# Memory layout of W_pe and p^T: one consecutive piece for each load

## The chip, the core and the metric

The kernel runs on one core of a Trainium2 chip. The metric is the device time of one execution in microseconds (us), lower is better. The core has a matrix engine (PE in the profile, its weight loads PEld), a vector engine (DVE), a scalar engine (ACT), a general engine (POOL), and SP, which here only issues DMAs. ACT can issue DMAs too. Every engine works through its own list of instructions in a fixed order and waits on semaphores for the others. PE reads its operands from on-chip memory (SBUF) and writes its sums to a second on-chip memory (PSUM), which the other engines read.

## The reference

One layer (DEPTH = 1) over 1024 tokens of 1024 numbers, in float32. What the change touches is the term with `p` and `w_ple_proj` (W_pe) in the last lines:

```python
h = rms_norm(x, norm_mix_g); proj = h @ w_in          # q, k, v, gates, conv inputs
o = gla_chunked(q, k, v, gk)                          # chunked gated linear attention
y_a = (rms_norm(o, gla_norm_g) * silu(z_a)) @ w_branch_a
u = causal_dwconv(cc * xc, conv_w)
y_c = (cb * u * silu(z_c)) @ w_branch_c
x = x + (sigmoid(g_a + b_ga) * y_a + sigmoid(g_c + b_gc) * y_c) @ w_out
ple_gate = sigmoid(rms_norm(x, norm_ple_g) @ w_ple_gate)
x = x + ple_gate * (p @ w_ple_proj)                   # p: 1024 x 256, w_ple_proj: 256 x 1024
return rms_norm(x, norm_final_g)
```

## The kernel before

Every float32 product is split into a high and a low part of a faster format (`split`, line 614: ACT casts the high part, DVE subtracts it for the low part) and made of three matmuls: high x high, high x low, low x high (`mm3`, line 625). The large products are further cut down by a seven-product scheme (class `Cell`, line 741). The program is not written in the order in which it runs. The functions note operations (`Flow.note`, line 260), and a planner (`set_dues`, `put_in_order`, lines 362 and 409) puts them in order for each engine by costs, latencies and due times; `nc.hurry` moves a due time forward. The cost of a DMA to the planner depends on its bytes alone. All operations are issued from line 520, so in the profile nearly every row carries L520 and is told apart by its tile's name.

The first thing that the kernel computes is the product p W_pe (`pe` in the profile), because it needs nothing but two small inputs: W_pe and p^T, 256 x 1024 each, 1 MB each. It is kept in memory (`ped`) until the last stage of the kernel, which loads it back and multiplies it by the gate. Eight matmuls on constants (`warm`, line 1049) run on PE while the first loads are on their way.

Before the change `_lay_out` (line 1839, on the host) hands both over as arrays of 128 x 2 x 1024: for each of the 128 rows of SBUF, the two blocks (`kt` = 0, 1) of 1024 numbers. Row after row is 8 KB on in memory, and a load of some columns of one block takes from each row a piece of 1 KB or 2 KB. The loads are, in the order of the program (lines 1069 to 1082; `first` names the first three pieces):

- two quarters of block 0, columns 0 to 255 and 256 to 511 (1 KB a row, 128 KB a load), W_pe's from ACT's queue, p^T's from SP's;
- block 1, columns 0 to 511 (2 KB a row, 256 KB), of W_pe and then of p^T, from SP's queue; called piece (1, first half) below;
- the second halves of W_pe's two blocks, from SP's queue;
- two loads of x^T (`hq`), then the second halves of p^T's two blocks, then two more of x^T.

The tiles that receive them are `wperaw` and `pTraw`; the split parts are `wpehi`, `wpelo`, `pThi` and `pTlo`. `pe_blocks` (line 1137) makes the products for token blocks 0 to 3 and the first 512 columns in two steps: first everything with block `kt` = 0, in the order of the quarters, for all four token blocks; then the rest with `kt` = 1, which needs the pieces (1, first half).

In the last stage (`make_gate`, line 1732) one part of p W_pe is computed a second time for the last rows instead of being loaded: `get` (line 1797) loads columns 256 to 511 of W_pe and the last 128 columns of p^T again into `pwraw`, splits them into `pwhi` and `pwlo`, and `piece` (line 1739) multiplies them into `pelast`. In the program and on SP's queue these loads stand some 66 us before their use.

Of the kernel before, what the change touches and what calls it, by code (L numbers as in the profile page):

```python
# [16 lines left out]
P = 128  # L17
# [519 lines left out]
def kernel(  # L537
# [4 lines left out]
    wb: bass.AP,  # L542
    wgl: bass.AP,
    wgk2: bass.AP,
    wpe: bass.AP,
    pT: bass.AP,
    xT: bass.AP,
    vecs: bass.AP,
    gbc: bass.AP,
# [3 lines left out]
    nc = Flow(tc)  # L553
# [57 lines left out]
    load = nc.sync.dma_start  # L611
    store = nc.sync.dma_start

    def split(hi, lo, src):

        nc.scalar.copy(hi, src)
        tt(lo, src, f(hi), op=ALU.subtract)
# [37 lines left out]
    def slot(k, s, name, shape=(4, 512), dtype=F32R):  # L655
        return rp.tile([P, *shape], dtype, tag=f"r{k}{s}", name=name)
# [84 lines left out]
    class Cell:  # L741
# [10 lines left out]
        def load(self, k):  # L752
            for n in NEED[self.side][k]:
                if self.raw[n] is None and not (self.fresh and k == 1 and n == 3):
                    self.raw[n] = bp.tile([P, 4, P], F32, tag="raw", name=f"{self.name}raw{n}", bufs=8)
                    load(self.raw[n], self.src[n])
            if k == 1 and self.s1 is not None and self.seed is None:
                self.seed = bp.tile([P, 512], F32, tag="raw", name=f"{self.name}s1", bufs=8)
                load(self.seed, self.s1)
# [142 lines left out]
    def rows(b):  # L902
        return slice(b * P, (b + 1) * P)
# [148 lines left out]
    with phase("prep0") as pool:  # L1052
        pr_ = slot(4, "h", "pTraw", (2, SEQ), F32)
        wr_ = slot(4, "l", "wperaw", (2, D), F32)
        halves = [slice(hh * 512, (hh + 1) * 512) for hh in range(2)]
# [7 lines left out]
        def get_x(i):  # L1063
            for n in (0, 3) if i == 0 else (1, 2):
                for kp in range(0, 4, 2):
                    kk = 4 * quad[n][1] + kp
                    load(q[n][:, kp:kp + 2, :], xT[:, kk:kk + 2, halves[i]])
# [2 lines left out]
        first = [(0, slice(0, 256)), (0, slice(256, 512)), (1, halves[0])]  # L1070
        for n, (kt, cs) in enumerate(first):
            nc.hurry = 14.0 - 2.0 * n
            (nc.scalar if kt == 0 else nc.sync).dma_start(wr_[:, kt, cs], wpe[:, kt, cs])
            load(pr_[:, kt, cs], pT[:, kt, cs])
        nc.hurry = 8.0
        for kt in range(2):
            load(wr_[:, kt, halves[1]], wpe[:, kt, halves[1]])
        nc.hurry = 0.0
        get_x(0)
        load(vec, vecs)  # L1080
        for kt in range(2):
            load(pr_[:, kt, halves[1]], pT[:, kt, halves[1]])
        get_x(1)
        load(trim, tri)

# [280 lines left out]
    with phase("conv", [ph["qk"]]) as vp:  # L1366
# [26 lines left out]
        for g in range(4):  # L1393
            t, u = [], []
# [269 lines left out]
    with phase("late", [ph["sw"], ep]) as lp:  # L1664
# [63 lines left out]
        with phase("fin", [ph["sw4"]], lp) as gp:  # L1728
# [3 lines left out]
            def make_gate(p, cell):  # L1732
# [56 lines left out]
                def late_cons(i, j, src):  # L1789
                    if not xt:  # L1790
                        get()
                    piece(i, slice(512 * j, 512 * j + 512), src, i ^ j, i != j)
# [4 lines left out]
                def get():  # L1797
                    for i in range(2):
                        xt.append(lp.tile([P, D], F32, tag="x", name=f"x3_{p}_{i}", bufs=4))
                        load(xt[i], x2d[2 * p + i])  # L1800
                        ms.append(sm.tile([P, 2], F32, tag="ms3", name=f"ms3_{p}_{i}", bufs=4))
                    if p == 3:
                        raw = gp.tile([P, 2, P + 256], F32, name="pwraw")
                        load(raw[:, :, 0:P], pT[:, :, rows(7)])
                        load(raw[:, :, P:], wpe[:, :, 256:512])
                        pw.extend(gp.tile([P, 2, P + 256], F32R, name=f"pw{s}") for s in ("hi", "lo"))
                        split(*pw, raw)

                def cons(i, j, src):
                    if p == 3 or p == 2 and i == 1:  # L1810
                        return late_cons(i, j, src)
                    if not xt:
                        get()
                    js = slice(j * 512, (j + 1) * 512)
                    t = gp.tile([P, 512], F32, tag="pe", name=f"pe{p}_{i}_{j}", bufs=4)
                    load(t, ped[2 * p + i][:, js])
                    act(src, src, AF.Sigmoid, scale=rgate[p, i][:, 0:1])
                    tt(t, src, t, op=ALU.mult)
                    tt(xt[i][:, js], xt[i][:, js], t, op=ALU.add)
                    act(junk[:, 0:512], xt[i][:, js], AF.Square, scale=1.0 / 32.0, accum_out=ms[i][:, j:j + 1])  # L1820
                    seen[i] += 1
                    if seen[i] == 2:
                        r = rstd_of(ms[i][:, 0:1], f"rf{p}_{i}", ms[i][:, 1:2])
                        stt(xt[i], xt[i], r[:, 0:1], gf, op0=ALU.mult, op1=ALU.mult)
                        store(out[rows(2 * p + i), :], xt[i])
# [13 lines left out]
def _lay_out(inp):  # L1839

    import numpy as np

    a = {n: np.asarray(v) for n, v in inp.items()}
    w = a["w_in"][0]
    o = np.cumsum([0, 512, 512, 1024, 1024, 16, 1024, 1024, 1024, 1024, 1024, 1024])
    q, k, v, za, gl, cb, cc, xc, zc, ga, gc = (w[:, o[i]:o[i + 1]] for i in range(11))
    col = lambda m, n: m[:, n * 256:n * 256 + 256]
    cells = []
    for hp in range(2):
        cells += [col(q, hp), col(k, hp)]  # L1850
    cells += [col(za, h) for h in range(4)]
    for g in range(4):
        cells += [col(m, g) for m in (cc, xc, zc, cb)]
    for m in (ga, gc, a["w_branch_c"][0], a["w_branch_a"][0]):
        cells += [col(m, c) for c in range(4)]

    def quads(m):
        n = m.shape[1] // 2
        t = lambda r, c: m[r * 512:r * 512 + 512, c * n:c * n + n].reshape(4, 128, n).transpose(1, 0, 2)
        return t(0, 0), t(0, 1), t(1, 1), t(1, 0)  # L1860

    wc = np.stack([np.stack([np.stack(quads(m)[0:2], 1), np.stack(quads(m)[2:4], 1)]) for m in cells])
    wb = np.stack([np.stack(quads(a[n][0])) for n in ("w_out", "w_ple_gate")] + [np.stack(quads(v))])
    pcol = lambda t: t.reshape(-1, 128).T
    vecs = np.concatenate([pcol(a["b_gk"][0]), pcol(a["b_merge"][0]),
                           a["conv_w"][0].reshape(3, 8, 128).transpose(2, 0, 1).reshape(128, 24),
                           pcol(a["norm_ple_g"][0]), pcol(a["norm_mix_g"][0]), pcol(a["gla_norm_g"][0])], axis=1)
    return {
        "x": a["x"][0],
        "wc": wc,  # L1870
        "wb": wb,
        "wgl": gl.reshape(8, 128, 16).transpose(1, 0, 2),
        "wgk2": np.concatenate([a["w_gk2"][0]] * 8),
        "wpe": a["w_ple_proj"][0].reshape(2, 128, 1024).transpose(1, 0, 2),
        "pT": a["p"][0, 0].T.reshape(2, 128, 1024).transpose(1, 0, 2),
        "xT": a["x"][0].T.reshape(8, 128, 1024).transpose(1, 0, 2),
        "vecs": vecs,
        "gbc": np.broadcast_to(a["norm_final_g"], (128, 1024)),
        "tri": np.triu(np.ones((128, 128), np.int32)),
    }  # L1880
# [20 lines left out]
```

## Time and profile before

| | us |
|---|---|
| median of 3 runs | 1098.43 |
| lowest, highest | 1097.17, 1099.57 |
| the profiled execution's own time | 1096.41 |
| its span, first to last instruction | 1094.6 |

| engine | busy us | share of the span |
|---|---|---|
| PE | 1086.2 | 99% |
| PEld | 905.5 | 83% |
| DVE | 854.0 | 78% |
| ACT | 601.1 | 55% |
| POOL | 56.5 | 5% |

Busy time is the union of an engine's instructions; issuing of DMAs and waiting are not in it. The span is that of one profiled execution, and 1.8 us of this execution's own time lie outside it. "Released by" in a row of the profile (`<-`) names what ended the idle time before an instruction, and an entry ending in q is the engine's own list of DMA issues (SPq, ACTq).

### The profile page before, as it was taken

The numbers are of one execution on the slowest core, as the hardware profiler recorded it, in microseconds if no ns is written. First come the engines' busy times: TensorE is split into PE (matmuls) and PEld (weight loads), VectorE is DVE, ScalarE is ACT, GpSimd is POOL, SyncE is SP. The second block draws the span as 40 slices with busy tenths as digits, with TensorE's granted clock in tenths as the row PEclk, the third lists the DMA queues.
The fourth block names the chain that finished last, engine by engine and source line by source line (L and its number), as shares of the span: only waits on it lengthen the run. The fifth ranks groups of instructions, "written<-read, shape, count | busy, mean of one in ns | idle before, by whom it ended". The sixth has DMA issues, their size and how long they took to land.

```text
span 1094.6 us, 15335 instructions
## 1 busy us (share of the span) xinstructions
PE 1086.2 (99%) x5042; PEld 905.5 (83%) x5042; DVE 854.0 (78%) x1391; ACT 601.1 (55%) x1115; POOL 56.5 (5%) x117
## 2 busy tenths in 40 slices
PE   9999999999999999999999999999999999999997
PEld 7888888888888888888888888888888888888886
DVE  6996477879878869748649677776999889959586
ACT  5875347876643454343334376766735445468554
POOL 0000000000000000000000022220000000001021
PEclk9999999999999999999999999999999999999999
DMA  9986463358877595212212699988695888889762
GB/s 306 359 274 213 158 199 113 110 180 258 251 231 244 184 294 193 99 58 68 87 58 73 217 305 338 339 264 274 193 345 163 307 264 284 302 299 314 272 221 101
DMA packets 157583, 241.18 MB, mean 220 GB/s; under 512 B 13504, under 2 KB 68416, under 8 KB 157504
## 3 DMA queue, kind: packets, MB, share of 16 engines
q1 hardware_dynamic: 157072, 239.75, 66.2%
q8 instruction: 39, 0.64, 0.2%
q10 hardware_dynamic: 432, 0.46, 0.1%
q14 instruction: 40, 0.33, 0.1%
HBM read 159.55 MB, written 80.61 MB: 219 GB/s over the span
## 4 chain that ended last, share of the span: by engine, by line
PE 98%; DMA 0%; DVE 0%; issue 0%; ACT 0%; POOL 0%; SPq 0%; POOLq 0%; ACTq 0%
PE vacc L520 7%; PE op L520 3%; PE X L520 2%; PE pe L520 2%; PE gc1Y L520 1%; PE ga3Y L520 1%; PE ga2Y L520 1%; PE gc0Y L520 1%; PE ga1Y L520 1%; PE out1Y L520 1%; PE ga0Y L520 1%; PE out3Y L520 1%; PE out2Y L520 1%; PE out0Y L520 1%; PE za2Y L520 1%; PE za0Y L520 1%
## 5 line engine op out<-in xcount | busy, mean ns | idle before, releaser
L520 ACT ACT_TABLE_LOAD x18 | 23.1, 1283 | 1.9 <-PEq L1890 1.6
L520 ACT ACTIVATE junk<-x 128x512 bf16<-128x512 f32 (+1 forms) x29 | 17.8, 613 | 8.3 <-DVE x L520 8.0
L520 DVE TENSOR_TENSOR wt<-wt 128x512 f32<-128x512 f32 x32 | 21.7, 686 | 0.8 <-DMA wtd<-wt 0.5
L520 POOL TENSOR_TENSOR or<-or,mhalf 128x1 f32<-128x1 f32 x32 | 20.6, 642 | 2.7
L520 DVE SCALAR_TENSOR_TENSOR u<-t,vec,u 128x1024 f32<-128x1024 f32 x16 | 20.4, 1277 | 0.0
L520 POOL MEMSET t<- 128x2 f32 x8 | 0.8, 100 | 377.6 <-DVE u L520 194.8
L520 ACT ACTIVATE og<-op,or 128x256 f32<-128x256 f32 x32 | 15.1, 471 | 7.7 <-POOL or L520 7.6
L520 DVE COPY_PREDICATED aT<-trim,X 128x128 f32<-128x128 int32 x32 | 9.6, 300 | 11.2 <-PE X L520 11.1
L520 POOL TENSOR_SCALAR rg<-ms 128x1 f32<-128x1 f32 x8 | 4.4, 556 | 260.0 <-ACT junk L520 260.0
L520 POOL TENSOR_SCALAR or<-oms 128x1 f32<-128x1 f32 x32 | 9.7, 303 | 124.6 <-ACT junk L520 124.5
L520 PE MATMUL op<-vl,aTh 128*128 128x256 f32 x64 | 15.2, 318 | 0.0
L520 PE MATMUL op<-Sh,qkl 128*128 128x256 f32 x56 | 14.6, 283 | 0.0
L520 DVE TENSOR_TENSOR szl<-op,szl 128x256 f32<-128x256 f32 x32 | 13.5, 423 | 1.3 <-PE op L520 0.7
L520 ACT CAST aTh<-aT 128x128 fp32r<-128x128 f32 x32 | 9.5, 297 | 8.3 <-DVE aT L520 7.9
L520 ACT ACTIVATE junk<-op 128x256 bf16<-128x256 f32 x32 | 12.3, 384 | 2.3 <-DVE szl L520 1.4
L520 PE MATMUL pe<-wpelo,pThi 128*128 128x512 f32 (+1 forms) x36 | 12.8, 374 | 0.7 <-DVE wpelo L520 0.7
L520 PE MATMUL pe<-wpehi,pThi 128*128 128x512 f32 (+1 forms) x36 | 13.0, 381 | 0.0
L520 PE MATMUL pe<-wpehi,pTlo 128*128 128x512 f32 (+1 forms) x36 | 13.0, 380 | 0.0
L520 PEld LDWEIGHTS X<-vl,keh 128*128 128x128 f32 x56 | 10.5, 188 | 2.4
L520 PE MATMUL X<-qkl 128*128 128x128 f32 x64 | 12.3, 273 | 0.0
L520 PE MATMUL op<-ident,og 128*128 128x128 f32 x64 | 12.3, 272 | 0.0
L520 DVE TENSOR_TENSOR Sl<-S,Sh 128x256 fp32r<-128x256 f32 x28 | 11.7, 418 | 0.3 <-ACT Sh L520 0.2
(3251 smaller groups left out, 4159.1 us busy)
## 6 DMA issues: line engine op xcount, KB each, us to landing
wtd<-wt SPq DMA_DIRECT2D x44, 256.0 KB, 3.9
qkl<-qkd SPq DMA_DIRECT2D x32, 320.0 KB, 5.0
wt<-in_wb_dram SPq DMA_DIRECT2D x8, 1024.0 KB, 6.5
vl<-vd SPq DMA_DIRECT2D x32, 256.0 KB, 4.7
vraw<-in_wb_dram SPq DMA_DIRECT2D x28, 256.0 KB, 4.3
wgq<-wtd SPq DMA_DIRECT2D x14, 512.0 KB, 7.3
uq<-ud SPq DMA_DIRECT2D x10, 512.0 KB, 6.2
oq<-od SPq DMA_DIRECT2D x10, 512.0 KB, 6.7
```

Source lines behind the costliest of these rows:

```text
L520: o.call(*[place(a) for a in o.args], **{k: place(a) for k, a in o.kw.items()})
```

## The change

`_lay_out` no longer hands over two arrays of 128 x 2 x 1024 but four: the two quarters of block 0 (`wpq`, `pTq`: 2 x 128 x 256) and the other three pieces (`wpo`, `pTh`: 3 x 128 x 512, in the order block 1 first half, block 0 second half, block 1 second half). Each load of the first stage then reads one consecutive piece of 128 KB or 256 KB, with 1 KB or 2 KB for each row as before. Number, size, order and queues of these loads stay: the quarters of W_pe go out from ACT's queue and all the rest from SP's, as they did. In the last stage the load of W_pe into `pwraw` becomes two loads of 128 KB, since its two blocks now lie in different arrays, and the planner puts p^T's load ahead of them.

```diff
@@ -1070,16 +1072,16 @@
         first = [(0, slice(0, 256)), (0, slice(256, 512)), (1, halves[0])]
         for n, (kt, cs) in enumerate(first):
             nc.hurry = 14.0 - 2.0 * n
-            (nc.scalar if kt == 0 else nc.sync).dma_start(wr_[:, kt, cs], wpe[:, kt, cs])
-            load(pr_[:, kt, cs], pT[:, kt, cs])
+            (nc.scalar if kt == 0 else nc.sync).dma_start(wr_[:, kt, cs], wpq[n] if n < 2 else wpo[0])
+            load(pr_[:, kt, cs], pTq[n] if n < 2 else pTh[0])
         nc.hurry = 8.0
         for kt in range(2):
-            load(wr_[:, kt, halves[1]], wpe[:, kt, halves[1]])
+            load(wr_[:, kt, halves[1]], wpo[1 + kt])
         nc.hurry = 0.0
         get_x(0)
         load(vec, vecs)
         for kt in range(2):
-            load(pr_[:, kt, halves[1]], pT[:, kt, halves[1]])
+            load(pr_[:, kt, halves[1]], pTh[1 + kt])
         get_x(1)
         load(trim, tri)
@@ -1801,8 +1803,9 @@
                     if p == 3:
                         raw = gp.tile([P, 2, P + 256], F32, name="pwraw")
-                        load(raw[:, :, 0:P], pT[:, :, rows(7)])
-                        load(raw[:, :, P:], wpe[:, :, 256:512])
+                        load(raw[:, :, 0:P], pTh[1:3, :, 384:512].rearrange("k p t -> p k t"))
+                        load(raw[:, 0, P:], wpq[1])
+                        load(raw[:, 1, P:], wpo[0, :, 256:512])
@@ -1865,14 +1868,19 @@
+    wpe, pT = a["w_ple_proj"][0].reshape(2, 128, 1024), a["p"][0, 0].T.reshape(2, 128, 1024)
+    quarters = lambda m: np.stack([m[0, :, 0:256], m[0, :, 256:512]])
+    others = lambda m: np.stack([m[1, :, 0:512], m[0, :, 512:1024], m[1, :, 512:1024]])
     return {
...
-        "wpe": a["w_ple_proj"][0].reshape(2, 128, 1024).transpose(1, 0, 2),
-        "pT": a["p"][0, 0].T.reshape(2, 128, 1024).transpose(1, 0, 2),
+        "wpq": quarters(wpe),
+        "wpo": others(wpe),
+        "pTq": quarters(pT),
+        "pTh": others(pT),
```

On PE, DVE, ACT and POOL the instructions and their order are the same before and after; on SP there is one more load, and the three loads into `pwraw` stand in another order.

More of the change, by code (lines that the diff above doesn't have):

```diff
@@ L544 @@
     wgk2: bass.AP,
-    wpe: bass.AP,
-    pT: bass.AP,
+    wpq: bass.AP,
+    wpo: bass.AP,
+    pTq: bass.AP,
+    pTh: bass.AP,
     xT: bass.AP,
```

## The prediction

> **What bounds the kernel now.** I read the page's busy times first, then the chain of work that ended last, then its first 12 us piece by piece.
>
> ```profile
> span 1094.6 us, 15335 instructions
> ...
> PE 1086.2 (99%) x5042; PEld 905.5 (83%) x5042; DVE 854.0 (78%) x1391; ACT 601.1 (55%) x1115; POOL 56.5 (5%) x117
> ...
> PE 98%; DMA 0%; DVE 0%; issue 0%; ACT 0%; POOL 0%; SPq 0%; POOLq 0%; ACTq 0%
> ```
>
> PE is busy for 99% of the span and is 98% of the chain. A layout of inputs can change the time only where PE is not busy, and the list of PE's waits has just two lines:
>
> ```profile
> PE warm L520 <- PEq L1890: 0.8, 1, 0.8
> PE pe L520 <- DVE wpelo L520: 0.7, 1, 0.7
> ```
>
> The first is the program's start. The second falls into the first product, p W_pe, and the chain's first pieces (start, us, what) say what is behind it:
>
> ```profile
> 2.11 5.40 DMA pTraw<-in_pT_dram
> 7.51 0.02 issue
> 7.53 0.44 DVE pThi L520
> ...
> 7.99 0.04 DVE pTlo L520
> ...
> 8.60 0.69 DVE wpelo L520
> ...
> 9.34 2.79 PE pe L520 x11
> ```
>
> SP issues p^T's piece (1, first half) at 2.11. It lands at 7.51; DVE makes three parts of it and of W_pe's piece, one after another, and PE goes on at 9.34. From there PE runs on to its last product. So the span hangs on this one landing: span = landing + 1.83 us of DVE + 1085.3 us (1094.6 - 9.34) that the change does not touch.
>
> **The change part by part.** *The first loads.* How much an earlier landing can bring is read from PE's rows in the timeline:
>
> ```profile
> 3.65 0.40 ACT L520 CAST wpehi<-wperaw 128x256 fp32r<-128x256 f32 x1 [0.72 <-DMA wperaw<-in_wpe_dram]
> 4.11 0.86 PE L520 MATMUL pe<-wpehi,pThi 128*128 128x256 f32 x2
> ...
> 5.62 0.63 PE L520 MATMUL pe<-wpehi,pThi 128*128 128x256 f32 x2
> ...
> 8.25 0.39 PE L520 MATMUL pe<-wpehi,pThi 128*128 128x512 f32 x1
> ...
> 9.21 1.34 ACT L520 CAST wpehi<-wperaw 128x512 fp32r<-128x512 f32 x2 [2.32 <-DMA wperaw<-in_wpe_dram]
> ...
> 9.34 0.50 PE L520 MATMUL pe<-wpelo,pThi 128*128 128x512 f32 x1 [0.70 <-DVE wpelo L520]
> 9.68 0.40 PE L520 MATMUL pe<-wpehi,pTlo 128*128 128x512 f32 x1
> 9.91 0.39 PE L520 MATMUL pe<-wpehi,pThi 128*128 128x512 f32 x1
> ```
>
> Two such matmuls in a row start 0.23 us apart (9.68, 9.91). The one at 9.34 could have started at 8.48: the wait costs 0.86 us, a little more than the 0.70 us that stand beside it, since a matmul's end is modelled. Landing x earlier gives x, up to 0.86 us; then PE's own work decides, which began at 4.11, right behind the warm-up matmuls. So earlier quarters bring almost nothing: at 4.11 the first two matmuls take 0.86 us where a later pair takes 0.63 (at 5.62), at most 0.2 us. The gain's bound is 0.86 + 0.2 = 1.06 us. What is late next is no limit: W_pe's second halves are read by ACT at 9.21, and PE needs them only after 11 more matmuls.
>
> Will the landing move? The table by stretches gives DMA share and GB/s in its last two columns:
>
> ```profile
> 1.70:4.40 2.70, 2.70 (x8) 0.90 (x7) 0.89 (x3) 1.65 (x3) 0.00 (x0) 1.00 0.88 285
> 4.40:8.40 4.00, 4.00 (x25) 3.92 (x24) 1.96 (x6) 1.01 (x2) 0.00 (x0) 1.00 0.93 265
> 8.40:12.40 4.00, 3.30 (x15) 2.55 (x14) 3.11 (x6) 2.79 (x4) 0.00 (x0) 1.00 1.04 389
> 12.40:14.00 1.60, 1.60 (x8) 1.31 (x7) 0.46 (x1) 1.44 (x2) 0.00 (x0) 1.00 1.07 406
> 26.00:30.00 4.00, 4.00 (x21) 3.29 (x19) 3.71 (x6) 2.75 (x5) 0.00 (x0) 1.00 0.98 387
> 56.00:58.00 2.00, 2.00 (x10) 1.65 (x10) 2.00 (x3) 2.00 (x4) 0.00 (x0) 1.00 0.71 185
> ```
>
> From 4.4 to 8.4, when the pieces (1, first half) come in, the DMA engines are as good as fully busy (0.93) but move only 265 GB/s, against 389 right after. There is something slow there. Is it the 8 KB from row to row? Two rows speak against it. From 12.4 to 14.0 the second halves of p^T land, laid out in just the same way, at 406 GB/s. And x^T, whose rows are 32 KB apart, makes up most of 8.4 to 12.4 at 389. Rows of x, which already are one consecutive piece for each load, make up most of 26 to 30: 387. A load by itself shows the same. `s1d` is consecutive, a weight cell (`ga0raw`) takes 2 KB every 4 KB, both 256 KB:
>
> ```profile
> ga1s<-s1d SPq DMA_DIRECT2D x1, 256.0 KB, 2.6
> ga0raw<-in_wc_dram SPq DMA_DIRECT2D x1, 256.0 KB, 2.6
> ```
>
> 2.6 us from issue to landing each. Bounds: if the stretch from 4.4 ran at 389 instead of 265 GB/s, the 3.11 us from 4.4 to 7.51 would be 3.11 x 265 / 389 = 2.12, and the landing 1.0 us earlier: the whole wait gone. If it ran at the slowest rate in the table, 185 GB/s, they would be 4.45 us and the landing 1.3 us later. I take 0.3 us earlier: nearest to the rows that show consecutive and strided alike (0), with a lean to the better side because 265 is already low beside its neighbours.
>
> The Trainium skill has a rule for this change and one against it. For: *DMA: Bandwidth & Descriptors*, "Latency and other measured facts", reports copies falling to half their rate at row pitches of 512 KiB to 8 MiB and advises to pad or to lay tiles out contiguously. By that rule read as holding at 8 KB too, the whole wait would go (rival one); the trace does not bear it out at 8 KB or at 32 KB (406 and 389 GB/s). Against: the same page, "Rules for kernel authors", holds that the tile in SBUF decides the number of descriptors; a tile of 128 rows has small ones for each row whatever the source. By that the sum would be 0.0. The trace agrees on the count before:
>
> ```profile
> DMA packets 702, 0.77 MB, mean 285 GB/s; under 512 B 70, under 2 KB 582, under 8 KB 702
> ```
>
> That is 582 - 70 = 512 packets of 1 KB from 1.7 to 4.4, 128 for each of the four quarters, one for each row of SBUF.
>
> *The last stage's loads.* One load more on SP, and another order:
>
> ```profile
> 1020.43 0.62 SPq L520 DMA_DIRECT2D pwraw<-in_wpe_dram  x1
> 1021.09 0.61 SPq L520 DMA_DIRECT2D pwraw<-in_pT_dram  x1
> 1021.80 1.49 SPq L520 DMA_DIRECT2D gt2raw<-gd  x3
> ...
> 1027.75 0.83 ACT L520 CAST pwhi<-pwraw 128x768 fp32r<-128x768 f32 x1
> 1029.46 0.62 ACT L520 CAST gt2hi<-gt2raw 128x512 fp32r<-128x512 f32 x1 [0.88 <-PE gt0X L520]
> L520 PEld LDWEIGHTS gt2X<-wg0hi,gt2hi x4: 188/188/188, 1048.3 to 1050.3; 128*128 128x128 f32 x4
> L520 PE MATMUL pelast<-pwhi x2: 280/281/282, 1086.8 to 1087.1; 128*128 128x256 f32 x2
> DMA to landing us min/median/max: 5.7/5.8/6.0
> ```
>
> An issue costs SP some 0.5 us (1.49 / 3). Behind it wait the loads `gt2raw` and `gt3raw`. The last line is the landing of the loads into `pwraw`: the third would now go out near 1021.7 and land by 1027.7, when ACT reads it (1027.75). If ACT had to wait 0.5 us, the 0.88 us of idle time ahead of its next cast would take it up. PE uses `gt2hi` only at 1048.3 and `pwhi` at 1086.8. Cost: 0; without this cover it would be 0.5 us.
>
> Sum against the profiled execution: its own time is 1096.41, 1.8 us more than its span; -0.3 + 0 gives 1096.1. The runs' median is 1098.43, 2.02 us above the profiled one, and their scatter is 2.4 us (1097.17 to 1099.57). Against the median: 1098.1. A measurement of this kernel tells about 0.2%, 2.2 us, from no change, and my whole gain is below half of that.
>
> **The rivals.**
>
> *One: the slow stretch is the layout's, and all of the wait goes.* For it: 265 GB/s only while W_pe and p^T are read side by side, two arrays of 1 MB at the same offsets. Against it: the 406 GB/s of the same layout. Gain 0.86 to 1.06 us, 1098.43 - 1.0 = 1097.4.
>
> *Two: the wait is longer in the runs without a profile, and goes.* The median is 2.02 us above the profiled execution, and the profile does not tell where. PE is packed from 9.34 on, so the first landing is a candidate. Then the wait there is 0.86 + 2.02 = 2.88 us, and without it the time is 1095.6, 0.26% faster. Against: nothing shows that the 2.02 us are there, and it needs rival one's mechanism as well.
>
> *Three: consecutive pieces crowd, and the landing comes later.* The rows that the 16 DMA engines read at one moment now lie 2 KB apart instead of 8 KB, all within 256 KB; if they get into each other's way, p^T's piece is late and PE stands still at 8.48 for as long. The 3.11 us after 4.4 carry 824 KB. To lose 2.2 us the rate has to fall under 824 / 5.31 = 155 GB/s, below the slowest row above (185, with a share of 0.71). At half the rate, 132 GB/s, the loss is 3.1 us: 1101.5. Against it: consecutive rows of x at 387 GB/s, and 2.6 us for `s1d`.
>
> *Four: nothing moves*, since packets, queues and order are the same: 1098.4.
>
> **How the numbers follow.** Forecast (landing within half a us of 7.2): 0.40, 1098.1. Rival one 0.20, two 0.17, three 0.13, four 0.10. The forecast and rivals one and four are all within 0.2%, save 0.03 of rival one and 0.01 of the forecast for the scatter of the medians. Faster by over 0.2%: 0.17 + 0.03 = 0.20. Slower by over 0.2%: 0.13 + 0.01 = 0.14. Within: 0.66. The range goes down to 1095.5, which takes in rival one with the scatter of the runs and the half of rival two that lies above its 1095.6, and up to 1100.6, the bound at 185 GB/s (1098.43 + 1.3) with some 0.9 us of scatter; it leaves out the other half of rival two and most of rival three.
>
> **What would show it.** In the changed kernel's profile the chain should again begin with the landing of p^T's piece (1, first half), between 6.7 and 8.0 us, and PE's wait for `wpelo` should be between 0 and 1.2 us. The rate from 4.4 to 8.4 decides between the cases: near 265 for the forecast and rival four, near 390 for rival one, under 155 for rival three. From 12 us to the end PE's rows should be the same, shifted. I would be wrong if PE showed a new wait behind 1020 us, if the number of 1 KB packets in the first 4.4 us changed from 512, or if the time moved by over 2.2 us with this landing where it was.

## The result: 1.5 us faster, and the profile after

| | us |
|---|---|
| before, median of 12 runs | 1097.07 (1096.38 to 1099.72) |
| after, median of 12 runs | 1095.58 (1095.13 to 1096.16) |
| ratio | 0.9981, interval 0.9972 to 0.9990 |
| profiled execution after: own time, span | 1095.63, 1093.8 |

The changed kernel is 1.49 us or 0.19% faster. The page, and the list of PE's waits under it:

```profile
span 1093.8 us, 15337 instructions
...
PE 99%; ACT 0%; DVE 0%; issue 0%; POOL 0%; POOLq 0%; ACTq 0%
...
PE warm L520 <- PEq L1898: 0.8, 1, 0.8
```

The wait for `wpelo` has left the list, and DMA has left the chain of waits, whose first pieces now belong to PE alone:

```profile
0.72 0.04 issue
0.76 3.57 PE warm L520 x8
4.33 9.87 PE pe L520 x49
```

The same stretches as before (DMA share and GB/s in the last two columns):

```profile
1.70:4.40 2.70, 2.70 (x8) 0.92 (x7) 0.94 (x3) 1.80 (x3) 0.00 (x0) 1.00 0.95 278
4.40:8.40 4.00, 4.00 (x25) 3.75 (x24) 2.82 (x8) 1.96 (x4) 0.00 (x0) 1.00 0.99 340
8.40:12.40 4.00, 4.00 (x18) 3.28 (x18) 2.71 (x5) 3.33 (x6) 0.00 (x0) 1.00 1.05 393
```

From 4.4 to 8.4 the DMA engines move 340 GB/s instead of 265, while their busy share rose only from 0.93 to 0.99. The timeline around p^T's piece (1, first half):

```profile
6.62 0.43 DVE L520 CAST pThi<-pTraw 128x512 fp32r<-128x512 f32 x1 [1.11 <-DMA pTraw<-in_pTh_dram]
...
7.69 1.88 DVE L520 TENSOR_TENSOR wpelo<-wperaw,wpehi 128x512 fp32r<-128x512 f32 x3
...
8.08 0.39 PE L520 MATMUL pe<-wpehi,pThi 128*128 128x512 f32 x1
...
8.43 0.50 PE L520 MATMUL pe<-wpelo,pThi 128*128 128x512 f32 x1
8.77 0.40 PE L520 MATMUL pe<-wpehi,pTlo 128*128 128x512 f32 x1
```

DVE starts on the piece at 6.62, where it started at 7.53 before. The matmul that needs `wpelo` starts at 8.43, where it started at 9.34. From 8.08 to 8.43 are 0.35 us where such a pair takes 0.23, so 0.12 us of wait is left. Behind it nothing differs: from there to the end are 1093.8 - 8.43 = 1085.4 us after and 1094.6 - 9.34 = 1085.3 before.

So PE's rows account for 0.9 us (8.43 against 9.34), and the medians of the runs differ by 1.5. Two questions are left. Is it the layout that brings the landing forward? And where do the other 0.6 us come from?

### The profile page after: what moved, and what is told of

Its sections match the earlier page's. It is cut to its first block, busy times and chain, and to the rows that moved or that the text cites. A ratio compares the mean times of both kernels' runs of the same rounds, so it can differ in the third digit from the quotient of the medians.

```text
span 1093.8 us, 15337 instructions
## 1 busy us (share of the span) xinstructions
PE 1086.0 (99%) x5042; PEld 905.4 (83%) x5042; DVE 853.7 (78%) x1391; ACT 600.4 (55%) x1115; POOL 56.8 (5%) x117
## 4 chain that ended last, share of the span: by engine, by line
PE 99%; ACT 0%; DVE 0%; issue 0%; POOL 0%; POOLq 0%; ACTq 0%
PE vacc L520 7%; PE op L520 3%; PE pe L520 2%; PE X L520 2%; PE gc1Y L520 1%; PE ga3Y L520 1%; PE ga2Y L520 1%; PE gc0Y L520 1%; PE ga1Y L520 1%; PE ga0Y L520 1%; PE out1Y L520 1%; PE out3Y L520 1%; PE out0Y L520 1%; PE out2Y L520 1%; PE za2Y L520 1%; PE za0Y L520 1%
```

## The experiments

Every comparison is with runs of the kernel before on the same chip: 1097.07, 1096.86, 1097.16 and 1097.00 us in the four sets that follow.

**The first loads or the last stage's.** `e1_first` makes the first loads consecutive and keeps `pwraw`'s loads as they were, from a second copy of both arrays. `e2_last` does the opposite.

```diff
 e1_first, against after
-                        load(raw[:, :, 0:P], pTh[1:3, :, 384:512].rearrange("k p t -> p k t"))
-                        load(raw[:, 0, P:], wpq[1])
-                        load(raw[:, 1, P:], wpo[0, :, 256:512])
+                        load(raw[:, :, 0:P], pT[:, :, rows(7)])
+                        load(raw[:, :, P:], wpe[:, :, 256:512])
 e2_last, against after: the first loads read wpe and pT (which stand behind the new arrays)
-            (nc.scalar if kt == 0 else nc.sync).dma_start(wr_[:, kt, cs], wpq[n] if n < 2 else wpo[0])
-            load(pr_[:, kt, cs], pTq[n] if n < 2 else pTh[0])
+            (nc.scalar if kt == 0 else nc.sync).dma_start(wr_[:, kt, cs], wpe[:, kt, cs])
+            load(pr_[:, kt, cs], pT[:, kt, cs])
...
```

> Only the first stage's loads are consecutive; the loads into pwraw read the old layout, with two DMAs, from a second copy of the arrays. Theory A (the first landing is what moved): like the changed kernel, ratio to the kernel before 0.998 (0.997 to 0.999), p^T's piece (1, first half) lands near 6.6 us and PE has no wait for wpelo. Theory B (the loads into pwraw, or their order on SP, are the gain): ratio 1.000, PE waits for wpelo about 0.9 us as before.

Measured: 1095.70 us (1095.34 to 1096.21), ratio 0.9984 (0.9976 to 0.9993).

> The complement: the first stage's loads are strided as before, the three loads into pwraw are those of the changed kernel. Theory A: ratio 1.000 (0.999 to 1.001), PE waits for wpelo 0.7 us or more, the landing is at 7.5 us or later. Theory B: ratio 0.998 with that wait unchanged.

Measured: 1096.12 us (1095.46 to 1097.54), ratio 0.9991 (0.9982 to 1.0000).

`e1_first` has 1.37 of the 1.49 us, so the first loads suffice for the gain. `e2_last` should have been as slow as before and was 0.95 us faster. Its trace shows that this isn't the last stage: its matmul for `wpelo` starts at 8.74, and from there to the end of its span are 1094.1 - 8.74 = 1085.4 us as in the other kernels. It is the first landing again, at 6.91, with strided loads. What differs from before in these loads is the place of the two arrays, which stand behind the new ones, 2 MB in all, in the list of arguments. The median hides two groups: seven of the eleven runs lie at 1095.46 to 1096.49 us, four at 1097.09 to 1097.54.

**More warm-up matmuls, to cover the landing.** 28 instead of 8, in both layouts. If the gain is only the wait, it should vanish.

```diff
-WARM = 8
+WARM = 28
```

> The kernel before with 28 instead of 8 warm-up matmuls, so that PE reaches block 1 near 12.7 us, later than any plausible landing of p^T's piece. About 3.6 us are added, near 1100 us. Theory A (the whole gain and the scatter of the kernel before come from the first landing): the scatter of 2 to 3 us between runs shrinks to under 1 us, and the time equals that of the next kernel within 0.1%. Theory C (the 2 us between the profiled execution and the median lie elsewhere): the scatter stays and this kernel stays about 0.1 to 0.2% above the next one.

Measured: 1103.37 us (1102.51 to 1104.66, 5 runs), ratio 1.0056 (1.0043 to 1.0068).

> The changed kernel with 28 warm-up matmuls; PE, DVE and ACT have the same order as in the kernel before with 28. Theory A: the same time as that one within 0.1%, both near 1100 us. Theory C: 0.1 to 0.2% faster than that one.

Measured: 1099.79 us (1099.41 to 1100.31), ratio 1.0023 (1.0014 to 1.0032).

Not equal, 3.6 us apart: the planner put the work in another order, and PE now waits for x^T further on. PE's waits of `e3_old_warm28`, and after the dots of `e4_new_warm28`:

```profile
PE ms L520 <- DVE sq L520: 1.4, 1, 1.4
...
PE ms L520 <- DVE sq L520: 0.5, 1, 0.5
```

That is 0.9 us of it. About 1.1 us more can't come from the loads: behind the same 28 matmuls on constants the first product starts at 9.12 us in the profile of `e3_old_warm28` and at 8.03 in that of `e4_new_warm28`. The largest part came out of the clock. In the old layout's stretches (granted clock in the third column from the end):

```profile
19.43:22.84 3.41, 2.00 (x13) 1.72 (x13) 3.38 (x7) 1.59 (x3) 0.00 (x0) 1.00 0.93 302
22.84:26.25 3.41, 3.41 (x10) 2.64 (x9) 2.14 (x4) 0.45 (x1) 1.33 (x1) 0.50 0.88 323
26.25:29.66 3.41, 3.41 (x21) 2.90 (x21) 2.20 (x4) 2.55 (x6) 0.00 (x0) 1.00 0.93 320
```

In the first stretch PE is busy for 2.00 of 3.41 us, because of the wait. In the next 3.41 us it is granted half the clock and does 10 matmuls where it then does 21. By these rows the stretch cost some half of 3.41, 1.7 us (an estimate), more than the wait itself. The three parts add up to 3.7 us; the two profiled executions differ by 3.4. The Trainium skill, *TensorE: Matmul & The Clock Gate*, section "What's actually happening", describes windows of 3413 ns after which the clock is set by the activity; the stretch here has that length. Its section on HAM oscillation states the rule as no idle gap over some 3.4 us. Here a wait of 1.4 us was followed by the half clock, and the measurement decides. The length of a wait alone doesn't settle it: `b2_before` (below) waits 0.9 and 0.8 us in close succession, and its granted clock is 1.00 from 8.4 to 12.4. The pair failed as a test of the cover, and showed a second price of a wait.

**Fill the wait without moving anything else.** Twelve matmuls on constants between block 0 and block 1 of `pe_blocks`, issued directly so that the planner's order stays. They take 2.64 us. If PE waits less than that in both layouts, the two kernels must become equal, and the time less 2.64 us is the time without any wait.

```diff
                 todo = todo[len(bs):]
+                nc.fill_at = len(nc.ops), warm[5], one
...
             for o in order:
+                if o.n == self.fill_at[0]:
+                    w, one = self.fill_at[1].place(), self.fill_at[2]
+                    for _ in range(12):
+                        self.tc.nc.tensor.matmul(w, one[:, 0:P], one, start=True, stop=True, skip_group_check=True)
                 o.call(
```

> The kernel before with 12 matmuls on constants between the products with block 0 and those with block 1; the order of all else is unchanged on every engine. They cost 12 x 0.227 = 2.7 us of PE and cover the wait. Theory A2 (all of the difference is PE's wait for the landing, and in the slowest runs of the kernel before the matmul clock falls back to half speed after that wait): no wait for wpelo, no second half-speed stretch, near 1098.5 us, the same as the next kernel within 0.1%. Theory C (the runs' difference lies elsewhere): 0.15% above the next one, as without the filler.

Measured: 1097.66 us (1097.27 to 1098.55), ratio 1.0006 (0.9997 to 1.0015).

> The changed kernel with the same 12 matmuls. Theory A2: within 0.1% of the kernel before with them. Theory C: 0.15% below it.

Measured: 1097.52 us (1097.13 to 1098.23), ratio 1.0006 (0.9997 to 1.0014).

Equal within 0.14 us (and some 0.9 us below the 1098.5 that was expected), and PE's list has only the program's start in both. The chain of `e5_fill_old`, all PE:

```profile
4.33 3.50 PE pe L524 x24
7.84 2.64 PE warm L523 x12
10.48 1.61 PE pe L524 x7
```

So the whole difference between the layouts is PE's wait at this place. And, if the twelve matmuls take 2.64 us in every run as they do in both profiles, it gives the size of the wait in the middle of the runs: before 1097.07 - (1097.66 - 2.64) = 2.05 us, after 1095.58 - (1097.52 - 2.64) = 0.70 us. In the profiled executions it was 0.86 and 0.12.

**Distance or layout.** `e7_old_moved` is the kernel before with an unused array of 2 MB ahead of W_pe, which moves both arrays. `e8_old_apart` has an unused array of 832 KB between the two, so that they no longer start 1 MB apart. Both keep the 8 KB from row to row.

```diff
 e7_old_moved, arguments (and the same place in _lay_out, 128 x 4096 zeros)
+    pad: bass.AP,
     wpe: bass.AP,
     pT: bass.AP,
 e8_old_apart, arguments (and the same place in _lay_out, 128 x 1664 zeros)
     wpe: bass.AP,
+    pad: bass.AP,
     pT: bass.AP,
```

> The kernel before with an unused array of 2 MB handed over ahead of W_pe, so that W_pe and p^T lie elsewhere in memory; layout and loads unchanged. Theory P (the place in memory decides, as the strided loads of e2_last were 0.9 us faster than in the kernel before): ratio 0.999, landing before 7.2 us. Theory L (the layout decides, the place does not): ratio 1.000.

Measured: 1096.82 us (1095.94 to 1098.96), ratio 1.0000 (0.9991 to 1.0009). p^T's piece lands at 7.90.

> The kernel before with an unused array of 832 KB between W_pe and p^T, so that the two no longer lie 1 MB apart. Theory S (the two streams get into each other's way because the same pieces lie 1 MB apart): 0.998, like the changed kernel, and the rate from 4.4 to 8.4 us goes to 340 GB/s or more. Theory L: ratio 1.000, rate near 265.

Measured: 1095.81 us (1095.36 to 1096.97), ratio 0.9988 (0.9979 to 0.9997). p^T's piece lands at 6.87.

Moving both does nothing. Moving them apart brings 1.05 us, without any consecutive load; this changes p^T's own place too, so distance and place aren't told from each other. Where the arrays really lie is in no trace: "moved" and "apart" speak of the list of arguments. The rate from 4.4 to 8.4 did not rise with it, though:

```profile
4.40:8.40 4.00, 3.46 (x24) 2.79 (x23) 2.44 (x7) 0.87 (x2) 0.00 (x0) 1.00 0.81 251
```

251 GB/s, though p^T's piece lands 0.64 us earlier than in the first profile of before, and W_pe's pieces come earlier as well. ACT starts on W_pe's piece (1, first half) at 5.33 instead of 6.26, and on W_pe's second halves at 8.44 instead of 9.21. The rate over a fixed stretch, which the prediction named as what decides, is a poor witness of one landing.

**The loads by themselves.** `m1_loads` leaves out everything but the ten first loads, and repeats them nine times for each of three layouts (A: strided, 1 MB apart; B: strided, 832 KB between; consecutive), with the same tiles, sizes and queues.

```diff
 for each repetition, the three sets in turn
+                yield nc.scalar, wq0[:, cs], w[:, 0, cs]
+                yield nc.sync, pq0[:, cs], p[:, 0, cs]
...
+            yield nc.sync, w1[:, :], w[:, 1, halves[0]]
+            yield nc.sync, p1[:, :], p[:, 1, halves[0]]
```

> The first loads by themselves, 9 times for each of three layouts in turn: strided with the two arrays 1 MB apart, strided with 832 KB between them, consecutive. Everything else of the kernel is left out. Theory L (the 8 KB from row to row is what slows the loads): p^T's piece (1, first half) takes as long in both strided sets, and 0.5 to 1.0 us less in the consecutive one. Theory S (two streams of rows that lie 1 MB apart get into each other's way): strided and apart is as fast as consecutive, strided with 1 MB is 0.5 to 1.0 us slower. Theory N (neither; the landing in the kernel varies from execution to execution by as much): the three medians lie within 0.3 us, with a scatter of 0.5 us or more from one repetition to the next.

Measured, in the list of DMA issues (`pone` is p^T's piece (1, first half), `wone` W_pe's, `wsecond` W_pe's second halves; median us from issue to landing at the end):

```profile
wsecond<-in_wA_dram SPq DMA_DIRECT2D x18, 256.0 KB, 6.3
wsecond<-in_wB_dram SPq DMA_DIRECT2D x18, 256.0 KB, 5.8
wsecond<-in_wo_dram SPq DMA_DIRECT2D x18, 256.0 KB, 5.5
...
wone<-in_wA_dram SPq DMA_DIRECT2D x9, 256.0 KB, 3.9
pone<-in_pA_dram SPq DMA_DIRECT2D x9, 256.0 KB, 5.3
...
wone<-in_wB_dram SPq DMA_DIRECT2D x9, 256.0 KB, 4.6
pone<-in_pB_dram SPq DMA_DIRECT2D x9, 256.0 KB, 4.9
...
wone<-in_wo_dram SPq DMA_DIRECT2D x9, 256.0 KB, 4.3
pone<-in_ph_dram SPq DMA_DIRECT2D x9, 256.0 KB, 5.0
```

For p^T's piece the three lie within 0.4 us, between theory S and theory N, and one repetition differs from another by up to 2.2 us (4.7 to 6.9 over all 27). W_pe's piece goes the other way: it is quickest in A. The order is clearer for all loads of W_pe and p^T together: the last of the eight lands, in the median, 9.56 us after a set's first issue in A, 8.87 in B, 8.39 in the consecutive set. So strided loads are slower as a whole, and part of that goes when the two arrays lie elsewhere and further apart; how much falls on p^T's piece this run doesn't settle.

**One array alone.** W_pe consecutive and p^T strided, then the reverse.

```diff
 e9_w_only, against after
-            load(pr_[:, kt, cs], pTq[n] if n < 2 else pTh[0])
+            load(pr_[:, kt, cs], pT[:, kt, cs])
...
 e10_p_only, against after
-            (nc.scalar if kt == 0 else nc.sync).dma_start(wr_[:, kt, cs], wpq[n] if n < 2 else wpo[0])
+            (nc.scalar if kt == 0 else nc.sync).dma_start(wr_[:, kt, cs], wpe[:, kt, cs])
...
```

> Only W_pe consecutive, p^T strided as before. Theory S: the two no longer walk through memory side by side, so all of the gain is there: 1095.6 to 1095.9, and no run of 1098 or more. Theory L: p^T's piece, which PE waits for, is as strided as before and lands about half as much earlier (W_pe's share of the traffic is half): about 1096.3. Theory N: between 1095.6 and 1097.1, with no relation to the layout.

Measured: 1096.08 us (1095.49 to 1097.67), ratio 0.9989 (0.9980 to 0.9997). p^T's piece lands at 6.53.

> Only p^T consecutive, W_pe strided as before. Theory S: all of the gain, 1095.6 to 1095.9. Theory L: half of it or a little more, since it is p^T's own piece: about 1096.1. Theory N: between 1095.6 and 1097.1, with no relation to the layout.

Measured: 1096.86 us (1096.24 to 1097.45), ratio 0.9995 (0.9986 to 1.0004). p^T's piece lands at 7.44.

With W_pe alone consecutive the time is 1.1 of the 1.5 us lower, although PE waits for p^T's piece; with p^T alone it is 0.3, not told from nothing. Theories S and L did not have the two so different; theory N allows it. Nor is the 1.1 shown to come from W_pe's layout: the strided array of these two kernels stands behind the new ones, as in `e2_last`, where both strided arrays were already 0.95 us faster. And `e9_w_only` falls into two groups like `e2_last`: seven runs at 1095.49 to 1096.10 us, four at 1096.80 to 1097.67. Both profiles show another wait, at the very first quarter; in `e9_w_only` and `e10_p_only`, in this order:

```profile
PE pe L520 <- ACT wpehi L520: 0.7, 1, 0.7
...
PE pe L520 <- ACT wpehi L520: 1.1, 1, 1.1
```

The first quarters land at 4.5 and 4.8 there, at 3.3 to 3.7 in both profiles of before and of after. Whether this is so in their other runs is open.

**Both remedies together, and a second profile of each kernel.** `e11_new_apart` is the changed kernel with the 832 KB between W_pe's and p^T's pieces; `b2_before` and `a2_after` are the two kernels themselves, profiled once more.

```diff
 e11_new_apart, against after (and the same place in _lay_out, 128 x 1664 zeros)
     wpo: bass.AP,
+    pad: bass.AP,
     pTq: bass.AP,
```

> The changed kernel with an unused array of 832 KB between W_pe's and p^T's pieces: consecutive and not 1 MB apart. If distance and layout are two causes of their own, both work here, PE hardly waits any more and the time is 1094.9 to 1095.3 (1097.52 less the 2.64 us that the twelve added matmuls cost when they filled the wait is 1094.9). If they are one cause, or if the time that is left is only the scatter of the first landing, it is the changed kernel's 1095.6.

Measured: 1095.74 us (1095.13 to 1096.20), ratio 0.9986 (0.9977 to 0.9995): the changed kernel's time. The two remedies don't add up. This fits one cause for both, and it fits two with a limit that either reaches; the run doesn't tell. No version that beats the changed kernel was found.

> The kernel before once more, for a second profile. Theory V (the landing varies, and the one profile of before happened to be a good one; its wait is about 2 us in the middle of its runs): p^T's piece lands between 7.0 and 9.0, anywhere but at 7.5 again to 0.2 us. Theory F (the landing is fixed by the layout): 7.5 within 0.2 us, and the rate from 4.4 to 8.4 near 265 GB/s.

Measured: 1096.90 us. PE's waits, the first pieces of the chain, and PE's timeline:

```profile
PE pe L520 <- DVE pThi L520: 0.9, 1, 0.9
PE pe L520 <- DVE wpelo L520: 0.8, 1, 0.8
...
2.11 5.82 DMA pTraw<-in_pT_dram
...
5.54 0.40 PE L520 MATMUL pe<-wpehi,pTlo 128*128 128x256 f32 x2
...
7.21 0.40 PE L520 MATMUL pe<-wpelo,pThi 128*128 128x256 f32 x2
8.53 0.47 PE L520 MATMUL pe<-wpehi,pThi 128*128 128x512 f32 x1 [0.92 <-DVE pThi L520]
9.77 0.50 PE L520 MATMUL pe<-wpelo,pThi 128*128 128x512 f32 x1 [0.77 <-DVE wpelo L520]
```

Here the wait is 2 us, in two pieces: PE could begin on block 1 at 7.45 (the last pair of block 0 starts at 7.21, and pairs start 0.24 us apart) and goes on without a stop only at 9.77. In the first profile a pair at 5.62 still took 0.63 us, here one at 5.54 takes 0.40. The first execution had spent a longer time at the start at the slow rate, so that PE came to block 1 only at 8.25, and its own slowness hid most of the wait. The rate from 4.4 to 8.4 is 285 GB/s in this profile.

> The changed kernel once more, for a second profile. Theory V: p^T's piece lands between 6.5 and 7.9. Theory F: 6.6 within 0.2 us, and the rate from 4.4 to 8.4 near 340 GB/s.

Measured: 1095.70 us; p^T's piece lands at 6.69, the rate from 4.4 to 8.4 is 328 GB/s.

Neither V nor F holds alone. The landings in all fifteen profiles of the whole kernel, sorted by what the first loads read, show a fixed part and some scatter:

| first loads | landing of p^T's piece (1, first half), us |
|---|---|
| strided, 1 MB apart: before, `b2_before`, `e3`, `e5`, `e7` | 7.51, 7.93, 7.90, 7.80, 7.90 |
| consecutive: after, `a2_after`, `e1`, `e4`, `e6` | 6.59, 6.69, 6.69, 6.56, 6.98 |
| strided, 832 KB between: `e8` | 6.87 |
| strided, one right behind the other, behind the new arrays: `e2` | 6.91 |
| consecutive, 832 KB between: `e11` | 6.10 |
| W_pe alone, p^T alone consecutive: `e9`, `e10` | 6.53, 7.44 |

The first two rows don't overlap; their middles are 7.90 and 6.69, 1.2 us apart. The first profile of before had the earliest landing of its five. But `e2` is strided and by its arguments 1 MB apart too, so it could stand in the first row, and then the rows do overlap.

The landing alone sets the time. In the eleven profiles of kernels without added matmuls, the execution's own time less the landing is between 1088.90 and 1089.04 us (before 1096.41 - 7.51, `b2_before` 1096.90 - 7.93, after 1095.63 - 6.59, `e10_p_only` 1096.40 - 7.44). So a time less 1089.0 is an estimate of the landing in runs without a profile. By the medians it is 8.1 before, 7.8 in `e7_old_moved`, 7.9 in `e10_p_only`, 7.1 in `e2_last` and `e9_w_only`, 6.8 in `e8_old_apart`, 6.7 in `e1_first` and `e11_new_apart`, 6.6 after. The 6.10 of `e11` is from its fastest run.

## Why the prediction was wrong

*The frame held.* The span is the landing plus 1.83 us of DVE plus a rest that nothing touches: `b2_before` 7.93 + 1.83 + 1085.3 = 1095.1, its span 1095.1; `e8_old_apart` 6.87 + 1.83 + 1085.3 = 1094.0, its span 1094.0; `e7_old_moved` 7.90 gives 1095.0, its span 1095.0. It was read from one chain and fits kernels that did not exist then. What it took for fixed is the chain's beginning: in the first profile after, the chain begins with PE's own work, not with the landing.

*The step that failed is the landing, taken as 0.3 us earlier.* It moved by 0.92 us between the first two profiles (to 6.59, ahead of the 6.7 to 8.0 that were announced), and by 1.2 between the middles of five each. The rows that argued for 0.3 were real, but of other company: from 12.4 to 14.0 p^T's second halves come in without W_pe beside them, and `s1d` and `ga0raw` were loads of one array. They show that rows 8 KB or 4 KB apart are not slow as such, which `e8_old_apart` bears out. They say nothing on two such arrays read side by side, and the only row that showed this was the slow one, 265 GB/s. Rival one named this condition and was given 0.20. In the first two profiles its gain came out, 0.91 of its 0.86 to 1.06 us, though at 340 GB/s and not at its 390.

*The second step that failed is the bound of 1.06 us.* It took the wait of one execution for the wait of all. The filled kernels give 2.05 us for the middle of the runs before, and `b2_before` shows the two pieces of it. The bound also took PE's arrival at block 1 as fixed, while it depends on how long the matmuls at the start run at the slow rate (0.63 or 0.40 us a pair at the same place).

*Rival two had the mechanism and, by luck, the time.* The wait is longer in most runs than in the first profile, and most of it goes. Its price was wrong: 2.88 us, because the whole 2.02 us between the profiled run and the median of three was put there. The measured wait is 2.05 us of which 0.70 is left, a gain of 1.35 by this reckoning and 1.49 by the medians. Its 1095.6 came from a higher starting value (1098.43; the twelve runs, with those three among them, gave 1097.07). The prediction also held that 2.2 us is the least that can be told from no change; the medians of twelve runs told 1.49 us.

*Where the 0.6 us beyond the two profiles come from.* About 0.3 is the first profile of before, with its early landing (1.2 against 0.92). The other 0.25 fits the clock: of 96 runs of before in the four sets, 19 have a mean granted clock of 0.996 or 0.997, and in the first set these six are at 1098.4 to 1098.9, the others at 1096.25 to 1097.88. Without the six the median there is 1096.82, that is 0.25 lower. A second stretch of 3.41 us at half the clock takes 0.5 x 3.41 / 1095 = 0.0016 from the mean clock and 1.7 us of time, which is how these runs lie. It isn't the only way to a long run: one of 1099.54 us in the second set has no lowered clock. None of the 24 runs of the changed kernel, `e1_first` and `a2_after` has a clock so low. That the stretch follows the first wait in these runs was seen in no trace of before; `e3_old_warm28` shows it behind another wait.

*Rivals three and four.* Crowding did not come: 340 GB/s, far above the 155 at which it would have cost 2.2 us. That nothing moves is out as well, by the 0.92 us of the landing.

*The last stage's loads cost nothing, as worked out.* SP in the profile after:

```profile
1019.04 0.53 SPq L520 DMA_DIRECT2D pwraw<-in_pTh_dram  x1
1019.61 0.55 SPq L520 DMA_DIRECT2D pwraw<-in_wpq_dram  x1
1020.25 0.41 SPq L520 DMA_DIRECT2D pwraw<-in_wpo_dram  x1
...
1026.93 0.83 ACT L520 CAST pwhi<-pwraw 128x768 fp32r<-128x768 f32 x1
1028.64 0.62 ACT L520 CAST gt2hi<-gt2raw 128x512 fp32r<-128x512 f32 x1 [0.88 <-PE gt0X L520]
```

The third issue takes 0.41 us, ACT reads 6.3 us behind it, without a stop, and its next idle time is the same 0.88 us as before. The packets of the first 4.4 us are as announced, 582 - 70 = 512 of 1 KB:

```profile
DMA packets 693, 0.75 MB, mean 278 GB/s; under 512 B 70, under 2 KB 582, under 8 KB 693
```

*On the rules.* The Trainium skill, *DMA: Bandwidth & Descriptors*, "Latency and other measured facts", pointed the right way with its advice to lay tiles out contiguously; its smallest pitch is 512 KiB, with 207 GB/s, and the half of that stands only at 4 and 8 MiB; here the pitch was 8 KB. That the number of descriptors stays, by "Rules for kernel authors", is true and was no argument: the 512 packets of 1 KB stayed 512, and the piece behind them still landed 0.92 us sooner.

*What stays open.* Why p^T's piece lands earlier. Consecutive pieces landed early in all five profiles. Strided arrays handed over one right behind the other landed late in five and early in one, `e2_last`. By the list of arguments the two arrays of `e2_last` and those of `e7_old_moved` lie alike, 2 MB further on than before, and yet the first was fast in seven runs of eleven and the second kept the time of before. So neither the layout nor the distance is shown to be the cause by itself, and the cause inside the memory is not named here. Shown is that the first loads bring the whole gain, that they do it through this one landing, and that consecutive pieces, or 832 KB between the strided arrays, made it early.

## What to carry to other kernels

When a stretch of loads has its DMA engines busy but moves less than the stretch beside it, compare it with stretches in which the same streams run together, not with the same load by itself; then try a consecutive layout, and a pad between the arrays. A wait near the start should be read from more than one profiled execution, or measured by filling it with work of a known length: the filled kernel's time less that work is the time without the wait. A wait of PE can cost more than its length: the 1.4 us in `e3_old_warm28` were followed by 3.41 us at half the clock.

## What the runs showed of the hardware

- Two strided streams from arrays handed over one right behind the other: landing 7.5 to 7.9 us in five profiles, 6.9 in a sixth (`e2_last`); with 832 KB between them 6.9 (`e8_old_apart`); consecutive pieces 6.6 to 7.0 (five profiles).
- In eleven profiles the kernel's time follows one landing one to one: time less landing is 1088.90 to 1089.04 us.
- A wait of 1.4 us was followed by 3.41 us at half the granted clock (`e3_old_warm28`).
- The slow rate at the program's start ends at different times in executions of the same kernel: a pair of matmuls at 5.6 us takes 0.63 us in one profile of before and 0.40 in the other.
